# Two-layer decoder trunk: weight parts split earlier in the opening, part of the gate's modulation on TensorE, rotary embedding in two operations

## Chip, cores and metric

One core of one Trainium2 chip. The time is device microseconds (us) of one execution, median of several runs. PE is TensorE's matmul stream, PEld its weight loads, DVE VectorE, ACT ScalarE, POOL GpSimd, SP the engine whose queue issues the weight transfers.

## What is computed

Two layers of a trunk for 256 tokens of width 1024. All six modulation vectors of a layer come from one vector `c`.

```python
mod = c_act @ w_ada[l] + b_ada[l]                 # 6 x 1024 values
sh_m, sc_m, gt_m, sh_f, sc_f, gt_f = split(mod)
h = rms_norm(x, g_pre_mix[l]) * (1 + sc_m) + sh_m
proj = h @ w_in[l]                                # q, k, v of two groups; indexer q, k, weights
y = concat(rms_norm(moba(...)), rms_norm(dsa(...))) @ w_out[l]
x = x + gt_m * rms_norm(y, g_post_mix[l])
h = rms_norm(x, g_pre_ffn[l]) * (1 + sc_f) + sh_f
y = (gelu(conv(h @ w_up_act)) * (h @ w_up_lin)) @ w_down
x = x + gt_f * rms_norm(y, g_post_ffn[l])
```

With 256 tokens the MoBA group (8 heads of 64) is plain causal attention; the DSA group (8 heads) keeps for each token the 64 best keys by an indexer's score. The rotary embedding turns the first 16 elements of each head of q and k: `x1*c - x2*s`, `x2*c + x1*s`.

## The kernel before

**Numbers.** Each matmul of a projection is three matmuls: every operand is split into a high part and a low part. For a weight, ACT makes the high part `wh` (L139, or L135 with a gain) and DVE the low part `wl` (L140, L136). `wh` and `wl` have five buffers each.

**Weights.** Everything comes in one stream, in the order of the program, by 1 MB transfers on SP's queue (`load`, L112) into six buffers `raw`. A transfer is issued when the tile that had its buffer has been read, and those behind it in the queue wait too.

**Modulation.** `gemv_v` (L182) does it on DVE: one multiplication with accumulation (L189) of 128x1024 weights by the row `crow` for each group of 128 outputs, 24 of them in the first mixer: groups 16 to 23 are the gate `gt_m`, 24 to 39 are `sh_f` and `sc_f`; 40 to 47 (`gt_f`) follow in the MLP. A generator yields its gap in ticks between them, and `Background.tick` advances all such chains once for each k step of a projection. A scheduler then sets the order on each engine, so that an instruction can stand far from its line; `pin` keeps an instruction in the program's order.

**Opening** (`start`, L576). The 1024 rows of the first projection come in eight steps k of 128. Step k gets shift and scale for its 128 channels (on DVE in `modulation_v`, L650; on PE in `modulation`, L659, for k = 0, 3, 6), splits the weight row in two parts of 584 and 1024 columns (`divide`, L634), modulates the transposed tokens on ACT into `hh` (L644) and `t` (L646), and DVE makes `hl` (L647). Then PE does the step's products (L695) for the indexer (`ia`, `ib`), `mq` and `mk`.

**First mixer.** PE projects `mv`, `dq`, `dk`, `dv` (`project`, L357, two token tiles t each, matmuls L369). Chains run beside it: transposes of q and k (`heads_T`, L342; `ki_T`, L754), the indexer (L393) with its top 64 on DVE (L419, L420), both attentions (`attend`, L427, scores on DVE at L449), then the output projection into four banks (L539 to L541). `gate_rows` (L202) turns the gate into a row for all partitions by a transpose and two transfers. `boundary` (L310) closes the mixer: `residual` (L296, L304) for each token tile, the next norm (L232, L264), transposes (L252) and the modulation (`mod_T`, L275 to L287), after which PE does the MLP.

Of the kernel before, what the change touches and what calls it, by code (L numbers as in the profile page):

```python
# [13 lines left out]
AF = mybir.ActivationFunctionType  # L14
OP = mybir.AluOpType
AX = mybir.AxisListType
# [58 lines left out]
def trunk(ctx: ExitStack, tc, plan, x, c, stream, small, rope, out):  # L75
    nc = tc.nc
# [7 lines left out]
    bg = Background()  # L84
# [62 lines left out]
    rt = con.tile([128, 2, 2, 16], F32, name="rt")  # L147
# [3 lines left out]
    ident = con.tile([128, 128], F32, name="ident")  # L151
# [5 lines left out]
    cs32 = con.tile([128, 8, 32], F32, name="cs32")  # L157
# [17 lines left out]
    mods = [con.tile([128, 48], F32, name=f"mod{l}") for l in range(DEPTH)]  # L175
# [6 lines left out]
    def gemv_v(l, j0, j1, gap, behind=None):  # L182

        for j in range(j0, j1, 2):
            r = load(("v_a", l, j, 2048))[0]
            for i in range(2):
                ri = r[:, 1024 * i:1024 * i + 1024]
                with tc.issue_after(behind) if behind else ExitStack():
                    nc.vector.scalar_tensor_tensor(out=ri, in0=ri, scalar=1.0, in1=crow, op0=OP.mult, op1=OP.mult,  # L189
                                                   accum_out=mods[l][:, j + i:j + i + 1])  # L190
                yield gap
        nc.vector.tensor_tensor(out=mods[l][:, j0:j1], in0=mods[l][:, j0:j1],
                                in1=scol(l, "b_ada")[:, j0:j1], op=OP.add)

    def pre_scale(l, which):
        a = wrk.tile([128, 8], F32, name="prescale", tag="prescale", bufs=2)
        o = 8 if which == "mix" else 32
        nc.vector.scalar_tensor_tensor(out=a, in0=mods[l][:, o:o + 8], scalar=1.0,
                                       in1=scol(l, "g_pre_" + which)[:, :8], op0=OP.add, op1=OP.mult)
        return a, mods[l][:, o - 8:o]  # L200
# [128 lines left out]
    def rope_out(p, dst, t, is_q, nh):  # L329

        nc.scalar.activation(out=dst, in_=p, func=AF.Copy, scale=0.125 if is_q else 1.0)
        n = wrk.tile([128, 8, 2, 16], F32, name="ra", tag="ra", bufs=2)[:, :nh]
        x = dst[:, :, :16]

        y = bass.AP(tensor=x.tensor, offset=x.offset + 8, ap=list(x.ap[:2]) + [[-8, 2], [1, 8]])
        cosv = rt[:, t, 0, :][:, None, :].to_broadcast([128, nh, 16])
        sinv = rt[:, t, 1, :].rearrange("p (a b) -> p a b", a=2)[:, None].to_broadcast([128, nh, 2, 8])
        nc.vector.tensor_tensor(out=n[:, :, 0], in0=x, in1=cosv, op=OP.mult)
        nc.vector.tensor_tensor(out=n[:, :, 1].rearrange("p h (a b) -> p h a b", a=2), in0=y, in1=sinv, op=OP.mult)
        nc.vector.tensor_tensor(out=x, in0=n[:, :, 0], in1=n[:, :, 1], op=OP.add)  # L340

    def heads_T(src, dst, t):  # L342
        yield 5
# [232 lines left out]
    def start():  # L576
# [48 lines left out]
        halves = half_T(0), half_T(1)  # L625
# [8 lines left out]
        def divide(k, u):  # L634
            w[k, u] = split(rows[k][:, 584:] if u else rows[k][:, :584], pin=True)

        def modulate(k):
            sk, mk = scale[:, k:k + 1], mods[0][:, k:k + 1]
            pin(nc.vector.scalar_tensor_tensor(out=sk, in0=mods[0][:, 8 + k:9 + k], scalar=plus1[:, k:k + 1],
                                               in1=scol(0, "g_pre_mix")[:, k:k + 1], op0=OP.add, op1=OP.mult))  # L640
            pin(nc.vector.tensor_tensor(out=mk, in0=mk, in1=scol(0, "b_ada")[:, k:k + 1], op=OP.add))
            divide(k, 0)
            xk = xT[k // 4][:, k % 4, :]
            pin(nc.scalar.activation(out=hh[:, k, :], in_=xk, func=AF.Identity, scale=sk, bias=mk))  # L644
            f = t2()[:, :S]
            pin(nc.scalar.activation(out=f, in_=xk, func=AF.Identity, scale=sk, bias=mk))  # L646
            pin(nc.vector.tensor_tensor(out=hl[:, k, :], in0=f, in1=hh[:, k, :].bitcast(F32), op=OP.subtract))  # L647
            divide(k, 1)

        def modulation_v(k):  # L650
            for a in range(2):
# [80 lines left out]
    for l in range(DEPTH):  # L732

        qiT = big("qT")
        kiT = wrk.tile([128, S], F32, name="kiT", tag="kiT", bufs=1)
# [18 lines left out]
        def ki_T(ki, t):  # L754
            p = tp_bank()
            nc.tensor.transpose(p[:, :128], ki, ident)
            nc.vector.tensor_copy(kiT[:, 128 * t:128 * t + 128], p[:, :128])
            yield 1

        def qk_done(dst, is_q):  # L760
# [25 lines left out]
            run_project("ib", lambda t, a: idx_out(1, t, a))  # L786
            st["behind"] = placed[0]
        if l == 0:
            bg.add("gt", gemv_v(l, 16, 24, 6))
        bg.add("gt", gate_rows(l, "mix"))  # L790
        if l:
            bg.add("sf", gemv_v(l, 32, 40, 6, placed[1][1]))
# [20 lines left out]
        bg.add("att", attend(mqT, mkT, mv, None, 0, oh, ol, ready[0]))  # L813
        dqT, dkT, dv = big("qT"), big("kT"), big("v")
        if l == 0:
            bg.add("sf", gemv_v(l, 24, 40, 9))
        run_project("dq", qk_done(dqT, True))
        run_project("dk", qk_done(dkT, False))
        bg.add("att", attend(dqT, dkT, dv, masks, 4, oh, ol, ready[1]))
# [135 lines left out]
def _layout(a, plan):  # L955

    parts = []
    for units in plan:
        blocks = []
        for kind, l, key, n in units:  # L960
            if kind == "v_a":
                w = a["w_ada"][l][:, 128 * key:128 * key + 256].reshape(128, 8, 2, 128)
                b = w.transpose(3, 2, 1, 0)
            elif kind in ("s", "sv"):
                b = a["w_ada"][l][:, :2 * D].reshape(128, 8, 2, 8, 128)[:, :, :, key]
                if kind == "sv":
                    b = b.transpose(3, 2, 1, 0)
            elif kind == "r":
                b = a["w_in"][l][128 * key:128 * key + 128, sum((CCOLS[n] for n in OPEN), [])]
            elif kind in "wb":  # L970
                name, k0, k = key
                w = a["w_in" if kind == "w" else "w_up_lin"][l].reshape(8, 128, -1)[k0:k0 + k]
                b = w[:, :, CCOLS[name]].transpose(1, 0, 2)
            elif kind == "o":
                b = a["w_out"][l][128 * key:128 * key + 128]
            elif kind in "uv":
                w = a["w_up_act" if kind == "u" else "w_up_lin"][l].reshape(8, 128, FF)
                b = w[:, :, 128 * key:128 * key + 128].transpose(1, 0, 2)
            else:
                b = a["w_down"][l][128 * key:128 * key + 128]  # L980
            blocks.append(b.reshape(128, n))
        parts.append((blocks[0] if len(blocks) == 1 else np.concatenate(blocks, axis=1)).reshape(-1))
    stream = np.concatenate(parts)
    assert stream.size == STREAM
    return stream
# [13 lines left out]
def _rope_table():  # L999
    f = np.float32  # L1000
    pos = np.arange(S, dtype=f)
    inv = f(500000.0) ** (-np.arange(0, 16, 2, dtype=f) / f(16))
    ang = pos[:, None] * inv[None, :]
    co, si = np.cos(ang).astype(f), np.sin(ang).astype(f)
    cc, ss = np.concatenate([co, co], 1), np.concatenate([-si, si], 1)
    tab = np.stack([cc, ss], axis=1)
    return np.ascontiguousarray(tab.reshape(2, 128, 2, 16).transpose(1, 0, 2, 3))

# [21 lines left out]
```

## Time and profile before

| what | value |
|---|---|
| median of 3 runs | 696.31 us (695.06 to 696.6) |
| profiled execution, own time | 694.81 us |
| its span, first to last instruction | 693.0 us |
| PE busy | 662.4 us (96%) |
| DVE busy | 560.6 us (81%) |
| ACT busy | 422.4 us (61%) |
| POOL busy | 31.8 us (5%) |
| granted TensorE clock, mean | 0.994 |

The profiled execution is 1.5 us shorter than the median. Busy time is the union of an engine's instructions; consecutive instructions on DVE overlap by some 0.08 us, and consecutive matmuls overlap as well, so that a busy PE need not be one that issues without a pause.

### The profile page before, as it was taken

How to read it: one execution, taken by the hardware profiler on the slowest of the kernel's cores; microseconds unless marked ns; L12 is line 12 of the kernel's file. 1: busy time of each engine (PE TensorE's matmuls, PEld its weight loads, DVE VectorE, ACT ScalarE, POOL GpSimd, SP SyncE). 2: the span in 40 equal slices, each digit the busy share in tenths (PEclk: the TensorE clock that was granted, in tenths of full speed). 3: DMA queues.
4: the chain of work that ended last, by engine and by line, in shares of the span. 5: the costliest groups of instructions: out<-in, count | busy, mean ns of one | idle time of the engine just before them, and what ended most of it. 6: DMA issues, size and time to landing. Idle time of an engine off the chain costs nothing.

```text
span 693.0 us, 11206 instructions
## 1 busy us (share of the span) xinstructions
PE 662.4 (96%) x4257; PEld 569.1 (82%) x4257; DVE 560.6 (81%) x1130; ACT 422.4 (61%) x781; POOL 31.8 (5%) x56
## 2 busy tenths in 40 slices
PE   7999988997999999999999998999999999999996
PEld 4777766775899999999988776877789999999994
DVE  5779999999799999988669996678679886666553
ACT  5446567994865555555565657879586555555441
POOL 1000001012000000000020000000100000000000
PEclk9999999999999999999999999999999999999998
DMA  8997963766479999998444933345336895555001
GB/s 363 419 363 269 404 244 130 295 216 249 155 288 360 375 375 335 338 337 316 167 171 177 348 124 122 122 155 200 132 150 228 302 341 187 220 183 183 1 1 61
DMA packets 24517, 163.02 MB, mean 235 GB/s; under 512 B 3312, under 2 KB 3728, under 8 KB 6160
## 3 DMA queue, kind: packets, MB, share of 16 engines
q1 hardware_dynamic: 23184, 159.77, 61.2%
q0 software_dynamic: 704, 2.11, 1.0%
q8 instruction: 33, 0.54, 0.3%
q10 hardware_dynamic: 576, 0.43, 0.2%
q14 instruction: 20, 0.16, 0.1%
HBM read 161.24 MB, written 1.06 MB: 234 GB/s over the span
## 4 chain that ended last, share of the span: by engine, by line
PE 67%; DVE 18%; ACT 9%; issue 4%; POOL 1%; DMA 1%; SPq 0%; POOLq 0%; DVEq 0%; ACTq 0%
PE b L540 18%; PE b L539 18%; PE b L541 18%; PE b L369 7%; DVE raw L189 4%; DVE wl L140 3%; ACT t L453 2%; DVE iscore L420 2%; PE b L695 2%; DVE iscore L412 2%; DVE tiny L419 1%; PE b L389 1%; ACT wh L135 1%; ACT t L232 1%; PE b L468 1%
## 5 line engine op out<-in xcount | busy, mean ns | idle before, releaser
L140 DVE TENSOR_TENSOR wl<-raw,wh 128x1024 fp32r<-128x1024 f32 (+1 forms) x146 | 173.6, 1195 | 34.7 <-ACT wh L139 30.9
L539 PE MATMUL b<-hh,wh 128*128 128x256 f32 x640 | 180.0, 281 | 0.0
L541 PE MATMUL b<-hl,wh 128*128 128x256 f32 x640 | 179.7, 281 | 0.0
L540 PE MATMUL b<-hh,wl 128*128 128x256 f32 x640 | 179.7, 281 | 0.0
L139 ACT ACTIVATE wh<-raw 128x1024 fp32r<-128x1024 f32 (+1 forms) x146 | 149.2, 1045 | 45.2 <-PE b L541 36.4
L540 PEld LDWEIGHTS b<-hh,wl 128*128 128x128 f32 x640 | 122.5, 191 | 1.4
L539 PEld LDWEIGHTS b<-hh,wh 128*128 128x128 f32 x640 | 120.3, 188 | 1.4
L541 PEld LDWEIGHTS b<-hl,wh 128*128 128x128 f32 x640 | 120.1, 188 | 0.0
L189 DVE SCALAR_TENSOR_TENSOR raw<-raw,crow 128x1024 f32<-128x1024 f32 x80 | 96.2, 1219 | 1.4 <-DMA raw<-in_stream_dram 1.4
L369 PE MATMUL b<-wh,hh 128*128 128x512 f32 (+1 forms) x184 | 72.7, 397 | 0.0
L369 PE MATMUL b<-wh,hl 128*128 128x512 f32 (+1 forms) x184 | 68.5, 386 | 0.0
L139 ACT ACTIVATE dh<-raw 128x1024 fp32r<-128x1024 f32 (+2 forms) x47 | 49.7, 1059 | 25.8 <-PE b L540 25.8
L140 DVE TENSOR_TENSOR dl<-raw,dh 128x1024 fp32r<-128x1024 f32 (+2 forms) x47 | 56.8, 1210 | 8.9 <-ACT dh L139 8.9
L912 ACT ACTIVATE t<-b,smt 128x256 f32<-128x256 f32 x44 | 25.1, 571 | 57.4 <-PE b L541 57.3
L539 PE MATMUL b<-dh,t 128*128 128x512 f32 x152 | 59.7, 393 | 0.0
L540 PE MATMUL b<-dh,t 128*128 128x512 f32 x152 | 59.6, 392 | 0.0
L541 PE MATMUL b<-dl,t 128*128 128x512 f32 x152 | 59.2, 389 | 0.0
L369 PE MATMUL b<-wl,hh 128*128 128x512 f32 (+1 forms) x184 | 55.2, 391 | 2.7 <-DVE wl L140 2.7
L369 PEld LDWEIGHTS b<-wl,hh 128*128 128x128 f32 x184 | 33.9, 189 | 10.8 <-DVE wl L140 4.0
L369 PEld LDWEIGHTS b<-wh,hh 128*128 128x128 f32 x184 | 34.6, 188 | 7.3 <-issue 1.0
L369 PEld LDWEIGHTS b<-wh,hl 128*128 128x128 f32 x184 | 33.8, 188 | 5.9
L913 DVE SCALAR_TENSOR_TENSOR t<-b,smt,t 128x255 f32<-128x255 f32 x44 | 21.1, 480 | 20.7 <-ACT t L912 20.6
(167 smaller groups left out, 1105.2 us busy)
## 6 DMA issues: line engine op xcount, KB each, us to landing
raw<-in_stream_dram SPq DMA_DIRECT2D x143, 1024.0 KB, 6.5
raw<-in_stream_dram SPq DMA_DIRECT2D x8, 804.0 KB, 8.2
gate<-gated POOLq DMA_DIRECT2D x4, 512.0 KB, 7.0
xt<-in_x_dram SPq DMA_DIRECT2D x2, 512.0 KB, 4.1
raw<-in_stream_dram SPq DMA_DIRECT2D x1, 984.0 KB, 5.9
out_dram<-xt SPq DMA_DIRECT2D x2, 256.0 KB, 2.1
raw<-in_stream_dram SPq DMA_DIRECT2D x1, 328.0 KB, 5.0
out_dram<-xt ACTq DMA_DIRECT2D x1, 256.0 KB, 2.1
```

The source lines that it names most:

```text
L139: put(nc.scalar.activation(out=hi[:, :n], in_=raw, func=AF.Copy))
L140: put(nc.vector.tensor_tensor(out=lo[:, :n], in0=raw, in1=hi[:, :n].bitcast(F32), op=OP.subtract))
L189: nc.vector.scalar_tensor_tensor(out=ri, in0=ri, scalar=1.0, in1=crow, op0=OP.mult, op1=OP.mult, accum_out=mods[l][:, j + i:j + i + 1])
L369: mm = lambda l_, k, i, start=False, stop=False: nc.tensor.matmul(a[:, :n], lhsT=l_[:, k, tt], rhs=w[k][i], start=start, stop=stop)
L412: nc.vector.scalar_tensor_tensor(out=sc, in0=r[:, j * nk:j * nk + nk], scalar=wi[:, h:h + 1], in1=fill[:, 256 - nk:] if first else sc, op0 ...
L420: nc.vector.match_replace(out=sc, in_to_replace=m8, in_values=sc, imm_value=MARK)
L453: nc.scalar.activation(out=ev[:, j, :], in_=ev[:, j, :], func=AF.Exp, bias=nm[:, j:j + 1], scale=-1.0, accum_out=sm[:, j:j + 1])
L539: nc.tensor.matmul(y, lhsT=hh, rhs=wh, start=first, stop=False)
L540: nc.tensor.matmul(y, lhsT=hl, rhs=wh, start=False, stop=False)
L541: nc.tensor.matmul(y, lhsT=hh, rhs=wl, start=False, stop=last)
L912: nc.scalar.activation(out=z, in_=p[:, :256], func=AF.Identity, scale=w2[:, i:i + 1], bias=bc[:, i:i + 1])
L913: nc.vector.scalar_tensor_tensor(out=z[:, 1:], in0=p[:, :255], scalar=w1[:, i:i + 1], in1=z[:, 1:], op0=OP.mult, op1=OP.add)
```

## The change

1. **Opening.** In steps 1 to 7 the second part of the weight row (1024 columns) is split ahead of the modulation of the tokens, so that ACT and DVE do both parts first. Step 0 keeps its order.
2. **First mixer's modulation.** Groups 24 to 31 take the gate's place in the early chain on DVE (gap 6). The gate (16 to 23) goes to PE: `gemv_p` waits 34 ticks, loads two 1 MB blocks, waits 16 ticks, and then does 16 matmuls (32 columns of `cs32` stationary, 256 columns of weights moving) in a row, a copy on ACT, four transposes, and a small reduction on DVE; twice. Groups 32 to 39 stay on DVE with gap 9.
3. **Rotary embedding.** One multiplication of twice the size makes both products, and the addition reads the second with its halves exchanged. Three DVE operations become two, 14 times in each layer.
4. **`ki_T`.** The copy of the indexer's transposed keys goes from DVE to ACT, twice in each layer.

```diff
+    def gemv_p(l, j0, j1, wait, gap):
+
+        yield wait
+        for j in range(j0, j1, 4):
+            r = [load(("p", l, j + 2 * i, 2048))[0] for i in range(2)]
+            yield gap
+            p = tp_bank()
+            burst([(p[32 * (i % 4):32 * (i % 4) + 32, 256 * h:256 * h + 256], cs32[:, i, :],
+                    r[h][:, 256 * i:256 * i + 256], dict(start=i < 4, stop=i >= 4, skip_group_check=True))
+                   for h in range(2) for i in range(8)])
+            e = t2()
+            nc.scalar.activation(out=e, in_=p, func=AF.Copy)
+            yield 4
+            q = tp_bank()
+            for b in range(4):
+                nc.tensor.transpose(q[:, 128 * b:128 * b + 128], e[:, 128 * b:128 * b + 128], ident)
+            nc.vector.tensor_reduce(out=mods[l][:, j:j + 4], axis=AX.X, op=OP.add,
+                                    in_=q.rearrange("p (b g r) -> p b g r", b=4, g=4)[:, :, :, 0])
+            yield 1
+        nc.vector.tensor_tensor(out=mods[l][:, j0:j1], in0=mods[l][:, j0:j1],
+                                in1=scol(l, "b_ada")[:, j0:j1], op=OP.add)
...
-        nc.vector.tensor_tensor(out=n[:, :, 0], in0=x, in1=cosv, op=OP.mult)
-        nc.vector.tensor_tensor(out=n[:, :, 1].rearrange("p h (a b) -> p h a b", a=2), in0=y, in1=sinv, op=OP.mult)
-        nc.vector.tensor_tensor(out=x, in0=n[:, :, 0], in1=n[:, :, 1], op=OP.add)
+        nc.vector.tensor_tensor(out=n, in0=x[:, :, None, :].to_broadcast([128, nh, 2, 16]),
+                                in1=rt[:, t][:, None].to_broadcast([128, nh, 2, 16]), op=OP.mult)
...
+        nc.vector.tensor_tensor(out=halves(x), in0=halves(n[:, :, 0]), in1=y, op=OP.add)
...
             divide(k, 0)
+            if k:
+                divide(k, 1)
             xk = xT[k // 4][:, k % 4, :]
...
-            divide(k, 1)
+            if k == 0:
+                divide(k, 1)
...
-            nc.vector.tensor_copy(kiT[:, 128 * t:128 * t + 128], p[:, :128])
+            nc.scalar.copy(kiT[:, 128 * t:128 * t + 128], p[:, :128])
...
         if l == 0:
-            bg.add("gt", gemv_v(l, 16, 24, 6))
+            bg.add("sf", gemv_v(l, 24, 32, 6))
+            bg.add("gt", gemv_p(l, 16, 24, 34, 16))
...
         if l == 0:
-            bg.add("sf", gemv_v(l, 24, 40, 9))
+            bg.add("sf", gemv_v(l, 32, 40, 9))
```

The layout of the gate's blocks in the stream and the sign in the table of sines follow. The moved instructions stand as follows (line numbers of each kernel's own file).

DVE in the opening, steps 1 and 2, before:

```order
L653 SCALAR_TENSOR_TENSOR raw,mod_99<-raw,crow 128x1024 x2
L639 SCALAR_TENSOR_TENSOR prescale<-mod_99,plus_161,smt 128x1
L641 TENSOR_TENSOR mod_99<-mod_99,smt 128x1
L140 TENSOR_TENSOR wl<-raw,wh 128x584
L647 TENSOR_TENSOR hl<-t_246,hh 128x256
L140 TENSOR_TENSOR wl<-raw,wh 128x1024
```

and now:

```order
L678 SCALAR_TENSOR_TENSOR raw,mod_99<-raw,crow 128x1024 x2
L661 SCALAR_TENSOR_TENSOR prescale<-mod_99,plus_161,smt 128x1
L663 TENSOR_TENSOR mod_99<-mod_99,smt 128x1
L140 TENSOR_TENSOR wl<-raw,wh 128x584
L140 TENSOR_TENSOR wl<-raw,wh 128x1024
L671 TENSOR_TENSOR hl<-t_250,hh 128x256
```

The low part of 1024 columns now stands between the parts that ACT works on and `hl`, which needs both of them.

PE in the first mixer, second token tile of `dq` (`b_864`, before `b_875`), where the indexer's second set of products follows (`kiT`, `qT`). Before:

```order
L369 MATMUL b_875<-wl,hh 128x512 x3
L389 MATMUL b_923<-kiT,qT 128x256
L389 MATMUL b_922<-kiT,qT 128x256
L389 MATMUL b_923<-kiT,qT 128x256
L389 MATMUL b_922<-kiT,qT 128x256
L369 MATMUL b_875<-wl,hh 128x512 x3
```

and now:

```order
L411 MATMUL b_909<-raw,cs_84 32x256 x16
L391 MATMUL b_864<-wl,hh 128x512 x3
L411 MATMUL b_932<-kiT,qT 128x256
L411 MATMUL b_931<-kiT,qT 128x256
L411 MATMUL b_932<-kiT,qT 128x256
L411 MATMUL b_931<-kiT,qT 128x256
L391 MATMUL b_864<-wl,hh 128x512 x5
L210 MATMUL b_980<-ident,t_926 128x128 x4
```

The first block of the gate stands ahead of these products, its transposes behind them; the second block stands in the first token tile of `dv` in the same way.

DVE at the end of the first mixer (`o` is the last attention output, `t<-b,gate` the residual's product). Before:

```order
L534 TENSOR_TENSOR hl<-o,hh 128x4x128
L189 SCALAR_TENSOR_TENSOR raw,mod_99<-raw,crow 128x1024 x3
L296 TENSOR_TENSOR t_1749<-b_1463,gate 128x512
L192 TENSOR_TENSOR mod_99<-mod_99,smt 128x16
L296 TENSOR_TENSOR t_1750<-b_1464,gate 128x512
L198 SCALAR_TENSOR_TENSOR prescale<-mod_99,smt 128x8
L304 SCALAR_TENSOR_TENSOR xt<-t_1749,tiny_1759,xt 128x512
L304 SCALAR_TENSOR_TENSOR xt<-t_1750,tiny_1759,xt 128x512
```

and now:

```order
L318 TENSOR_TENSOR t_1778<-b_1504,gate 128x512
L556 TENSOR_TENSOR hl<-o,hh 128x4x128
L189 SCALAR_TENSOR_TENSOR raw,mod_99<-raw,crow 128x1024
L140 TENSOR_TENSOR wl<-raw,wh 128x1024
L318 TENSOR_TENSOR t_1779<-b_1505,gate 128x512
L326 SCALAR_TENSOR_TENSOR xt<-t_1778,tiny_1788,xt 128x512
L326 SCALAR_TENSOR_TENSOR xt<-t_1779,tiny_1788,xt 128x512
L189 SCALAR_TENSOR_TENSOR raw,mod_99<-raw,crow 128x1024
```

Three modulation instructions are gone from between `hl` and the residual. The two that now stand here are the first of groups 40 and 41, which before stood a little later, between the second token tile's products and `mod_T`; one `wl` of the next projection has come here too.

## Rows read from the trace of the kernel before

**Rows 1.** Windows by stage: busy us (count) by engine, granted clock, DMA share, GB/s.

```profile
0.00:57.77 57.77, 50.49 (x282) 36.97 (x282) 40.21 (x82) 31.33 (x56) 2.88 (x12) 1.00 0.96 379
57.77:112.50 54.73, 48.57 (x274) 37.07 (x272) 54.44 (x178) 35.47 (x70) 1.31 (x2) 1.00 0.65 253
112.50:163.55 51.05, 50.10 (x314) 38.28 (x314) 49.29 (x118) 40.28 (x96) 10.15 (x6) 1.00 0.74 270
163.55:183.32 19.77, 15.22 (x68) 12.11 (x69) 14.88 (x29) 14.87 (x37) 3.12 (x6) 0.91 0.28 104
```

**Rows 2.** Timeline of DVE, opening, step 1: start, us, instruction, idle before and its releaser.

```profile
17.50 0.76 DVE L140 TENSOR_TENSOR wl<-raw,wh 128x584 fp32r<-128x584 f32 x1
18.75 0.42 DVE L647 TENSOR_TENSOR hl<-t,hh 128x256 fp32r<-128x256 f32 x1 [0.49 <-ACT t L646]
19.70 1.23 DVE L140 TENSOR_TENSOR wl<-raw,wh 128x1024 fp32r<-128x1024 f32 x1 [0.53 <-ACT wh L139]
...
23.46 0.76 DVE L140 TENSOR_TENSOR wl<-raw,wh 128x584 fp32r<-128x584 f32 x1
```

**Rows 3.** Timeline of ACT, opening, start of step 2.

```profile
23.58 0.60 ACT L644 ACTIVATE hh<-xT,mod,prescale 128x256 fp32r<-128x256 f32 x1 [3.33 <-DVE mod L641]
```

**Rows 4.** Timeline of PE, opening: first products of steps, a modulation, the mixer's start.

```profile
18.28 0.42 PE L695 MATMUL b<-wh,hh 128*128 128x328 f32 x1
...
41.30 0.42 PE L695 MATMUL b<-wh,hh 128*128 128x328 f32 x1
...
42.57 1.07 PE L664 MATMUL b<-raw,cs 128*32 128x256 f32 x16
...
47.41 0.31 PE L695 MATMUL b<-wh,hh 128*128 128x328 f32 x1
...
49.19 0.50 PE L695 MATMUL b<-wl,hh 128*128 128x512 f32 x1 [0.30 <-DVE wl L140]
...
52.44 0.42 PE L695 MATMUL b<-wh,hh 128*128 128x328 f32 x1
...
57.77 0.39 PE L369 MATMUL b<-wh,hh 128*128 128x512 f32 x1
```

**Rows 5.** PE's waits from 57.77 to 112.6 us: total, times, longest.

```profile
PE b L369 <- DVE wl L140: 2.7, 3, 1.6
PE b L346 <- DVE t L340: 1.4, 2, 0.9
```

**Rows 6.** Groups of DVE, 57.77 to 163.55 us: busy us, mean ns of one, idle before.

```profile
L189 DVE SCALAR_TENSOR_TENSOR raw<-raw,crow 128x1024 f32<-128x1024 f32 x24 | 28.8, 1220 | 0.0
...
L494 DVE TENSOR_TENSOR t<-t 128x256 f32<-128x256 f32 x2 | 0.8, 419 | 0.0
```

**Rows 7.** Timeline of DVE, first mixer: two operations of the rotary embedding.

```profile
62.53 0.28 DVE L338 TENSOR_TENSOR ra<-t,rt 128x128 f32<-128x128 f32 x1
62.73 0.29 DVE L340 TENSOR_TENSOR t<-ra 128x128 f32<-128x128 f32 x1
```

**Rows 8.** Timeline of DVE, end of the first mixer.

```profile
161.51 0.69 DVE L296 TENSOR_TENSOR t<-b,gate 128x512 f32<-128x512 f32 x1
...
162.87 0.75 DVE L304 SCALAR_TENSOR_TENSOR xt<-t,tiny,xt 128x512 f32<-128x512 f32 x1
...
168.81 1.21 DVE L189 SCALAR_TENSOR_TENSOR raw<-raw,crow 128x1024 f32<-128x1024 f32 x1
```

**Rows 9.** Timeline of PE, end of the first mixer: transposes and the waits before them.

```profile
155.37 0.32 PE L528 MATMUL b<-ident,tiny 128*128 128x128 f32 x1 [0.81 <-POOL tiny L525]
...
166.80 1.97 PE L252 MATMUL b<-ident,t 128*128 128x128 f32 x8 [3.26 <-DVE t L264]
...
175.22 1.10 PE L252 MATMUL b<-ident,t 128*128 128x128 f32 x8 [0.39 <-DVE t L264]
```

**Rows 10.** Window of two us after that wait (columns as in rows 1).

```profile
167.00:169.00 2.00, 2.00 (x9) 1.87 (x9) 2.00 (x5) 1.04 (x3) 0.56 (x1) 0.50 0.02 8
```

**Rows 11.** Weight transfers issued from 60 to 130 us: issue to landing, min, median, max.

```profile
DMA to landing us min/median/max: 4.7/6.7/8.3
```

More of the change, by code (lines that the diff above doesn't have):

```diff
@@ L333, in rope_out @@
         x = dst[:, :, :16]
-        y = bass.AP(tensor=x.tensor, offset=x.offset + 8, ap=list(x.ap[:2]) + [[-8, 2], [1, 8]])
-        cosv = rt[:, t, 0, :][:, None, :].to_broadcast([128, nh, 16])
-        sinv = rt[:, t, 1, :].rearrange("p (a b) -> p a b", a=2)[:, None].to_broadcast([128, nh, 2, 8])
-        nc.vector.tensor_tensor(out=n[:, :, 0], in0=x, in1=cosv, op=OP.mult)
-        nc.vector.tensor_tensor(out=n[:, :, 1].rearrange("p h (a b) -> p h a b", a=2), in0=y, in1=sinv, op=OP.mult)
-        nc.vector.tensor_tensor(out=x, in0=n[:, :, 0], in1=n[:, :, 1], op=OP.add)
+        nc.vector.tensor_tensor(out=n, in0=x[:, :, None, :].to_broadcast([128, nh, 2, 16]),
+                                in1=rt[:, t][:, None].to_broadcast([128, nh, 2, 16]), op=OP.mult)
+        y = n[:, :, 1]
+        y = bass.AP(tensor=y.tensor, offset=y.offset + 8, ap=list(y.ap[:2]) + [[-8, 2], [1, 8]])
+        halves = lambda v: v.rearrange("p h (a b) -> p h a b", a=2)
+        nc.vector.tensor_tensor(out=halves(x), in0=halves(n[:, :, 0]), in1=y, op=OP.add)
     def heads_T(src, dst, t):
@@ L963, in _layout @@
                 b = w.transpose(3, 2, 1, 0)
+            elif kind == "p":
+                b = a["w_ada"][l][:, 128 * key:128 * key + 256].reshape(128, 8, 256)
             elif kind in ("s", "sv"):
@@ L1004, in _rope_table @@
     co, si = np.cos(ang).astype(f), np.sin(ang).astype(f)
-    cc, ss = np.concatenate([co, co], 1), np.concatenate([-si, si], 1)
+    cc, ss = np.concatenate([co, co], 1), np.concatenate([si, -si], 1)
     tab = np.stack([cc, ss], axis=1)
```

## Prediction

> **What bounds the kernel now.** I read the windows by stage first, then the timelines of the engines that are full there, then the waits. Over the whole span PE is 96% busy, so a change helps where PE stands still or where another engine paces it. Rows 1 give four stages. In the opening (to 57.77 us) PE is busy 50.49 us and DVE 40.21, though it is the stage in which weights come at 379 GB/s. In the first part of the mixer (`mv`, `dq`, `dk` and the indexer, to 112.50) DVE is busy 54.44 of 54.73 us and PE only 48.57. In the second part (to 163.55) both are nearly full, PE 50.10 and DVE 49.29 of 51.05. At the boundary (to 183.32) PE is busy 15.22 of 19.77, at a mean granted clock of 0.91 [rows 1].
>
> What paces the opening shows on DVE: a step lasts from 17.50 to 23.46, 5.96 us, of which 0.49 is a wait for `t` from ACT and 0.53 one for `wh` from ACT; the work is 4.94 [rows 2]. ACT for its part stands 3.33 us until DVE has the next step's modulation [rows 3]. The two hand the step back and forth, and neither is full. PE follows them.
>
> **The opening: −3.8 us.** With both low parts ahead of `hl`, DVE works on 1024 columns (1.23 us) while ACT makes `hh` (0.60) and `t`, and ACT has split those columns while DVE did the 584. Both waits go, so DVE needs 4.94 us for a step. Then PE is next: from 41.30 to 47.41 a step with a modulation on PE took 6.11 us (two times eight matmuls of the modulation lie in such a step, 1.07 us for each eight), from 47.41 to 52.44 one without took 5.03, of which 0.30 is a wait, so 4.7 of work [rows 4]. From the start of step 1 at 18.28, five steps of 4.7 and two of 6.1 are 35.7 us, which puts the start of `mv` at 54.0 instead of 57.77 [rows 4]. If DVE's 4.94 holds in the five and PE's sequence has gaps, 1.3 to 1.8 less is gained; if PE's step has slack I don't see, a little more: ends −4.5 and −2.
>
> **First part of the mixer: 0.** Here two things are set against each other. PE stands still for 54.73 − 48.57 = 6.16 us [rows 1], of which 2.7 is waiting for a low part of a weight and 1.4 for rotated heads, both from DVE [rows 5]. DVE is relieved. Ahead of the first low part of `dv` stand 11 modulations by the new order, 13 by the old: two of 1.22 fewer, 2.4 [rows 6]. Fourteen rope operations go at a pitch of 0.20 each (62.53 to 62.73) [rows 7], but the product that replaces them is twice as wide: the nearest row is an operation of 128x256 at 0.42 against 0.28 for 128x128 [rows 6, 7], so 0.14 is paid and 0.06 saved, 14 times 0.8. Two copies of `ki_T` are bounded by the same pitch, 0.4, and a small reduction takes 0.1 back. Together 3.5 us. But the modulations used to fill DVE's time while the indexer waits for its scores; with fewer of them there, I expect most of it (2.7 to 3.5) to return as idle time of DVE. And PE gets the first burst: 16 matmuls of 256 columns at about 1.0 us for eight [rows 4] are 2.0 to 2.1, and the four transposes and the change of stationary operands 0.8 (a modulation step's 6.11 less 4.7 less 1.07 leaves 0.4 for two) [rows 4], together 2.8. It falls into PE's 6.16 of idle time where this lies near, else on the path. Ends −3.4 (the whole relief) and +2.8 (the whole burst); I take 0, since the indexer's chain and not DVE's sum decides here.
>
> [...]
>
> **Second part: +2.0.** PE is busy 50.10 of 51.05 us [rows 1], so the second burst's 2.8 lies on the path. What it may displace is the wait of 0.81 at 155.37 for a small operand from POOL [rows 9], which is over earlier when PE comes later: 2.8 − 0.8. Behind the burst on ACT stand a copy and the split of the output weights; if a transfer they wait for has been issued late, the landing of 4.7 (the least of [rows 11]) comes on top: ends +1.9 and +7.5.
>
> **Boundary: −3.4.** Between `hl` of the last output and the residual DVE has three modulations less. The last sum stands at 162.87, 1.36 behind the first product at 161.51 [rows 8], and one modulation and a `wl` are still there, which the new order puts ahead of the second product only; I take −1.4. One modulation at 168.81 of 1.21 [rows 8], ahead of `mod_T`, is moved off: −1.1, the pitch. And PE's wait of 3.26 before the first transposes is followed by 1.97 us for eight of them, the second eight taking 1.10 [rows 9]; the granted clock from 167 to 169 is 0.50, the lower level, after that wait [rows 10]. With a shorter wait I take the difference of 0.9 as gained. Ends −5 (all of it and a part of the remaining wait) and −0.5 (the moved instructions only change place).
>
> **Layer 1: −0.4.** The rope and the copies relieve DVE by 1.3 us as above; PE is nearly always full in that mixer, so a third of it. Ends −1.1 and 0.
>
> **Sum.** −3.8 + 0 + 2.0 − 3.4 − 0.4 = −5.6. The profiled execution would go from 694.81 to 689.2; the median of the runs lies 1.5 above the profiled one, so the median from 696.31 to **690.7**.
>
> **Rivals.**
> - *DVE paces the first mixer throughout.* For it: 54.44 of 54.73 busy. Then the relief of 3.5 shows in full and the burst falls wholly into PE's idle time, and about 1.1 more comes from the second part; the gain is 10.2 and the time 686.1. Against it: more than half of PE's idle time there is not put down to a low part [rows 5]. Chance 0.15.
> - *The stream bounds the opening.* The DMA share is 0.96 at 379 GB/s [rows 1]. If weights land just in time, a faster step only waits for its weights: the −3.8 goes, and with a little of the rest the time is 694.5. Against it: 57.77 us at 379 GB/s are 21.9 MB, while the tokens (1.05 MB), eight steps (0.82 and 1.05 each) and `mv` (2.1) need 18.1; the stream is 3.8 MB ahead, 10 us at that rate. Chance 0.07. [...]
> - *The longer ring, slower than before.* The four 1 MB blocks of the gate are held from their load through a wait of 16 ticks, two at a time, so that four buffers instead of six serve all else, and `dv` comes later in the stream. A transfer that waits for a buffer holds up the whole queue behind it; where a late landing is at the head of an in-order engine (ACT's split of the output weights behind the second burst, DVE's low parts before the boundary), each costs 4.7 to 8.3 us [rows 11]. It ends slower than before once such waits exceed 5.6 and the change's own uncertainty, some 7 us in all. Two such landings of 4.7 give 9.4 − 5.6 = +3.8, 700.1. Against it: the DMA share in these parts is 0.65 and 0.74 [rows 1], so the stream has room to catch up. Chance 0.10.
> - *The mixer gives the opening back.* Both bursts lie on the path (5.6) and the boundary gains only 1: −3.8 + 2.8 + 1.9 − 1.0 − 0.4 = −0.5, about 695.8. Chance 0.08.
>
> **How the numbers follow.** The forecast has 0.60. Its own range, from the ends of the terms taken a part at a time, is 687 to 694. The range is 685.0 to 696.5: below it takes in the rival in which DVE paces all, above it the stream and the mixer that gives the opening back; what is left out is the longer ring and a tenth of the others. A measurement of this kernel can tell about 0.2%, 1.4 us. Faster by more than this are the forecast and the first rival and most of the stream's case: 0.81 (0.60 + 0.15 + 0.06); within it lie the mixer that gives back and the rest, 0.09; slower is the longer ring, 0.10.
>
> **What would show it.** In the opening, DVE without the two waits in steps 1 to 7 and the start of `mv` near 54; if it stays near 57, the stream or PE's order is the bound. In the first part, PE's idle time between `mv` and the first low part of `dv`, and whether DVE now has idle time that it had not. The bursts at about 2.1 us each, with what PE did just ahead and behind; a burst that waits for its block would be the longer ring. At the boundary, the residual's last sum within 1.5 us of its first product, no modulation ahead of `mod_T`, the granted clock of the first transposes, and the MLP's start, 183.32 before, near 178. It is wrong if the opening gains under 2, if a landing shows as the releaser of a wait of over 2 us in the mixer, or if DVE fills the mixer and PE's idle time goes altogether.

## The result, and the profile after

| | kernel before | changed kernel |
|---|---|---|
| median, runs on the same chip | 695.06 us | 690.69 us (690.61 to 692.22, 5 runs) |
| ratio, 95% interval | | 0.9939 [0.9924, 0.9955] |
| profiled execution, span | 693.0 us | 688.8 us |
| PE busy, DVE busy | 662.4, 560.6 us | 665.3, 551.5 us |

The change saves 4.4 us by the medians and 4.2 us by the two spans. The forecast was 690.7 us from a median of 696.31; the kernel before took 695.1 to 695.3 in the runs beside which everything below was timed, so the forecast gain of 5.6 was 1.2 too large and the start 1.2 too high. Which terms of the sum hold is seen by stage.

The windows by stage of the changed kernel (start:end, length, then busy us and count of PE, PEld, DVE, ACT, POOL, granted clock, DMA share, GB/s); they answer to [rows 1], with the same borders: `mv`'s first product, the first product of `dv` with a low part, the last output product, the MLP's first product.

```profile
0.00:52.75 52.75, 48.74 (x281) 37.52 (x282) 39.25 (x90) 31.26 (x55) 2.88 (x12) 1.00 0.98 399
52.75:108.41 55.66, 51.68 (x309) 38.02 (x308) 52.29 (x150) 34.02 (x69) 0.00 (x0) 1.00 0.74 273
108.41:162.39 53.98, 53.08 (x351) 39.58 (x351) 46.98 (x113) 46.16 (x108) 6.34 (x9) 1.00 0.68 255
162.39:178.88 16.49, 14.11 (x69) 10.98 (x69) 12.11 (x25) 12.87 (x33) 3.05 (x6) 1.00 0.25 93
```

| stage | before | after | difference | forecast |
|---|---|---|---|---|
| opening | 57.77 | 52.75 | −5.0 | −3.8 |
| first part of the mixer | 54.73 | 55.66 | +0.9 | 0 |
| second part | 51.04 | 53.98 | +2.9 | +2.0 |
| boundary | 19.78 | 16.49 | −3.3 | −3.4 |
| the rest, layer 1 in it | 509.68 | 509.92 | +0.2 | −0.4 |
| span | 693.0 | 688.8 | −4.2 | −5.6 |

DVE's timeline in the opening, step 1 (start, us, instruction; idle time before it in brackets), answers to [rows 2]:

```profile
17.51 1.90 DVE L140 TENSOR_TENSOR wl<-raw,wh 128x584 fp32r<-128x584 f32 x2
19.32 0.42 DVE L671 TENSOR_TENSOR hl<-t,hh 128x256 fp32r<-128x256 f32 x1
...
22.27 1.90 DVE L140 TENSOR_TENSOR wl<-raw,wh 128x584 fp32r<-128x584 f32 x2
```

Both low parts now stand in one row, neither of the two waits of half a microsecond is left, and the step takes 4.76 us instead of 5.96. PE paces the opening instead. Its timeline there, first products of steps 3 to 6, answers to [rows 4]:

```profile
28.94 0.31 PE L720 MATMUL b<-wh,hh 128*128 128x328 f32 x1
...
33.33 0.31 PE L720 MATMUL b<-wh,hh 128*128 128x328 f32 x1
...
37.71 0.32 PE L720 MATMUL b<-wh,hh 128*128 128x328 f32 x1
...
43.51 0.31 PE L720 MATMUL b<-wh,hh 128*128 128x328 f32 x1
```

A step without a modulation is 4.39 us, one with it 5.80. The stream of weights is close behind: from 10 to 50 us it moves 418 GB/s, and ACT now waits three times for a weight to land (1.9 us in all, the longest below), which it never did in the opening before. PE is not held up by it, with 38.43 of 40.00 us busy.

```profile
10.00:50.00 40.00, 38.43 (x233) 31.39 (x231) 32.50 (x66) 24.40 (x41) 0.00 (x0) 1.00 1.02 418
```

```profile
29.36 1.65 ACT L139 ACTIVATE wh<-raw 128x584 fp32r<-128x584 f32 x2 [0.90 <-DMA raw<-in_stream_dram]
```

The bursts on PE, in the timeline of PE:

```profile
80.47 1.93 PE L411 MATMUL b<-raw,cs 128*32 128x256 f32 x32
...
85.57 0.60 PE L210 MATMUL b<-ident,t 128*128 128x128 f32 x4
...
91.03 0.44 PE L368 MATMUL b<-ident,t 128*128 128x128 f32 x2 [1.72 <-DVE t L362]
...
110.47 1.93 PE L411 MATMUL b<-raw,cs 128*32 128x256 f32 x32
...
163.81 1.09 PE L274 MATMUL b<-ident,t 128*128 128x128 f32 x8 [1.42 <-DVE t L286]
```

Neither burst waits for its block. The last row answers to the first two of [rows 9]: the wait ahead of the first transposes is 1.42 instead of 3.26 us, and the eight take 1.09 instead of 1.97; the granted clock of the boundary is 1.00, where it was 0.91.

What had not been there is idle time of DVE in the mixer. DVE, 64 to 71 us:

```profile
64.34 1.23 DVE L189 SCALAR_TENSOR_TENSOR raw<-raw,crow 128x1024 f32<-128x1024 f32 x1
...
68.37 2.36 DVE L140 TENSOR_TENSOR wl<-raw,wh 128x1024 fp32r<-128x1024 f32 x2 [2.79 <-ACT wh L139]
```

and ACT, which makes those high parts, at the same time:

```profile
65.82 0.60 ACT L795 ACTIVATE v<-b 128x512 f32<-128x512 f32 x1 [1.27 <-PE b L391]
66.31 0.58 ACT L369 COPY qT<-b 128x512 f32<-128x512 f32 x1
66.78 0.60 ACT L369 COPY kT<-b 128x512 f32<-128x512 f32 x1
67.25 1.08 ACT L139 ACTIVATE wh<-raw 128x1024 fp32r<-128x1024 f32 x1
```

The weights for `dq` stand on ACT behind three copies of PE's results, of which the first waited 1.27 us for PE. DVE has done all that it was given and stands still for 2.79 us, and it needs the time later: from there to the end of its indexer work (the second mask) it is busy 38.21 of 38.79 us. The mask, in the second row below, ends at 107.16, only 1.5 us earlier than the 108.63 of the kernel before, although `mv` starts 5.0 us earlier.

```profile
68.37:107.16 38.79, 35.25 (x212) 25.22 (x214) 38.21 (x124) 23.75 (x47) 0.00 (x0) 1.00 0.67 242
```

```profile
106.73 0.43 DVE L446 TENSOR_TENSOR mask<-mask,lateneg 128x256 f32<-128x256 f32 x1
```

### The profile page after: what moved, and what is told of

Same layout as the page of the kernel before. It is cut to its first block, busy times and chain, and to the rows that moved or that the text cites. A ratio compares the mean times of both kernels' runs of the same rounds, so it can differ in the third digit from the quotient of the medians.

```text
span 688.8 us, 11311 instructions
## 1 busy us (share of the span) xinstructions
PE 665.3 (97%) x4329; PEld 570.3 (83%) x4329; DVE 551.5 (80%) x1085; ACT 424.8 (62%) x787; POOL 26.6 (4%) x56
## 4 chain that ended last, share of the span: by engine, by line
PE 75%; DVE 11%; ACT 7%; issue 3%; POOL 1%; DMA 1%; SPq 0%; POOLq 0%; DVEq 0%; ACTq 0%
PE b L563 18%; PE b L562 18%; PE b L561 18%; PE b L391 11%; DVE wl L140 3%; PE b L720 3%; PE b L411 2%; ACT t L475 2%; DVE iscore L442 1%; PE b L490 1%; DVE tiny L441 1%; ACT t L254 1%; DVE iscore L434 1%; DVE raw L678 1%; DMA raw<-in_stream_dram 1%
## 5 line engine op out<-in xcount | busy, mean ns | idle before, releaser
L189 DVE SCALAR_TENSOR_TENSOR raw<-raw,crow 128x1024 f32<-128x1024 f32 x72 | 86.8, 1220 | 0.4 <-DMA raw<-in_stream_dram 0.2
```

## The experiments

Twelve kernels ran, in three groups of four. The first question was whether the parts of the change add, each in its own stretch (theory A), or whether the mixer takes the opening's gain back (B) or is paced by DVE (C). Ratios are against the kernel before, beside the same runs. The stages are of each kernel's profiled execution: "to the mask" is from `mv`'s first product to the end of the second mask on DVE, "to the outputs" from there to the last output product.

| kernel | median us | ratio, interval | `mv` at | to the mask | to the outputs | boundary | rest |
|---|---|---|---|---|---|---|---|
| before | 695.1 to 695.3 | | 57.77 | 50.86 | 54.91 | 19.8 | 509.7 |
| changed | 690.69 | 0.9939 [0.9924, 0.9955] | 52.75 | 54.41 | 55.23 | 16.5 | 509.9 |
| opening only | 694.53 | 0.9984 [0.9974, 0.9994] | 52.90 | 54.61 | 55.11 | 18.2 | 511.8 |
| gate only | 693.08 | 0.9965 [0.9953, 0.9978] | 57.73 | 50.30 | 57.81 | 15.8 | 509.4 |
| changed, gate on DVE | 695.99 | 1.0011 [0.9997, 1.0024] | 53.07 | 55.60 | 56.00 | 20.2 | 513.9 |
| changed, old rotary and copy | 690.64 | 0.9925 [0.9913, 0.9936] | 53.00 | 54.32 | 55.62 | 15.8 | 509.4 |
| changed, old opening | 696.45 | 1.0011 [1.0002, 1.0020] | 57.83 | 50.62 | 59.58 | 15.6 | 511.1 |
| rotary and copy only | 696.81 | 1.0019 [1.0005, 1.0032] | 57.73 | 53.15 | 60.47 | 15.1 | 510.1 |
| changed, earlier modulation | 689.08 | 0.9908 [0.9892, 0.9924] | 53.04 | 53.89 | 55.11 | 15.4 | 509.9 |
| changed, later burst | 692.37 | 0.9961 [0.9944, 0.9978] | 52.74 | 52.42 | 60.17 | 15.0 | 509.8 |
| opening, earlier modulation | 692.09 | 0.9959 [0.9948, 0.9971] | 53.01 | 52.92 | 56.09 | 18.5 | 511.6 |
| changed, gap 5 | 689.39 | 0.9919 [0.9907, 0.9931] | 52.87 | 53.37 | 55.76 | 15.7 | 509.9 |
| changed, gaps 5 and 13 | 689.20 | 0.9920 [0.9907, 0.9933] | 52.69 | 52.19 | 56.06 | 15.6 | 510.0 |
| copy only | 694.64 | 0.9996 [0.9982, 1.0009] | 57.73 | 51.30 | 57.46 | 15.3 | 509.8 |

A profiled execution can lie off the median of its kernel. That of "changed, gate on DVE" was the longest of its twelve, 4.5 us above their median, so its stages are too long in all; "opening, earlier modulation" lies 1.8 and "rotary and copy only" 1.6 above, "copy only" 1.2 below. The others lie within 0.8.

### The opening alone

```diff
             divide(k, 0)
+            if k:
+                divide(k, 1)
...
-            divide(k, 1)
+            if k == 0:
+                divide(k, 1)
```

> The kernel before with the opening's new order alone. Theory A, the parts act each in its own stretch and their gains add: mv starts near 52.75 us as in the changed kernel (57.77 before), and nearly all of the 5.0 us reaches the end, so the time is 4 to 5 us under the kernel before, about 0.993 of it, with the boundary still lasting 19.8 us and the transposes there at the lower clock. Rival B, the first mixer gives the opening back whoever makes it earlier (its modulations and weights come no sooner, so PE waits for them): mv near 52.75 but the output projection starts no more than 2.5 us earlier than 129.99, and the time is 0 to 2.5 us under the kernel before.

Measured: `mv` at 52.90, the time 0.6 us under the kernel before, 0.9984 of it. Theory A is gone: of 4.9 us at `mv`, 1.1 are left at the second mask (107.51 against 108.63), 0.9 at the last output product, 2.5 at the MLP's first product and by the span 0.4 at the end. Rival B's numbers hold (0 to 2.5, and the output projection starts 1.9 earlier), but not its reason: of 4.7 us of PE's waits up to the mask, 4.2 are put down to DVE and 0.5 to a weight's high part on ACT. DVE's side, by windows from `mv` to the mask, before and here:

```profile
57.77:108.63 50.86, 46.51 (x254) 35.70 (x254) 50.84 (x167) 31.60 (x58) 1.31 (x2) 1.00 0.70 272
```

```profile
52.90:107.51 54.61, 49.65 (x254) 36.40 (x254) 52.55 (x157) 33.57 (x60) 1.31 (x2) 0.95 0.72 268
```

PE does the same 254 matmuls, 3.1 us slower, with a mean granted clock of 0.95 (the last section has the place; DVE was busy throughout it, so the mask was not held up by it). DVE was busy 50.84 of 50.86 us before; here it is busy 52.55 of 54.61: 1.7 us of work more in that stretch (among it one modulation more ahead of the mask by the instructions' order, 13 for 12), and 2.06 idle, nearly all of it one wait:

```profile
68.73 2.36 DVE L140 TENSOR_TENSOR wl<-raw,wh 128x1024 fp32r<-128x1024 f32 x2 [1.95 <-ACT wh L139]
```

Together 3.75 of the 4.87 us gained. The boundary gave 1.6 us, and the MLP took 2.1 back: PE waits once, at its beginning, for DVE, where it did not before. On DVE a low part more stands ahead of each of the two operations that this matmul needs (`t`, L916 and L918; before, L913 and L915); first PE, then DVE, then DVE before:

```profile
188.53 0.36 PE L539 MATMUL b<-hh,wh 128*128 128x256 f32 x1 [1.58 <-DVE t L918]
```

```profile
185.20 1.22 DVE L140 TENSOR_TENSOR wl<-raw,wh 128x1024 fp32r<-128x1024 f32 x1
186.34 0.48 DVE L916 SCALAR_TENSOR_TENSOR t<-b,smt,t 128x255 f32<-128x255 f32 x1
186.77 1.23 DVE L140 TENSOR_TENSOR wl<-raw,wh 128x1024 fp32r<-128x1024 f32 x1
187.91 0.48 DVE L918 SCALAR_TENSOR_TENSOR t<-b,smt,t 128x254 f32<-128x254 f32 x1
```

```profile
187.92 0.48 DVE L913 SCALAR_TENSOR_TENSOR t<-b,smt,t 128x255 f32<-128x255 f32 x1
188.43 0.48 DVE L915 SCALAR_TENSOR_TENSOR t<-b,smt,t 128x254 f32<-128x254 f32 x1
```

The second of them comes 7.1 us after the MLP's first product, and 5.1 before. Of the fourteen kernels three have this wait, 1.58 or 1.60 us long: the three with the new opening and the gate on DVE.

### The gate alone

`gemv_p`, its two places in the chains and its blocks in the stream as in the change, all else as before.

> The kernel before with the gate's modulation on PE alone. Theory A: mv starts at 57.8; the mixer from there to the last output product becomes 2 to 4 us longer (PE work of 6.1 us comes in, of which the old idle time takes 2 to 4), the boundary 3.3 shorter than 19.8 us; the time is between 1.5 under and 1 us over the kernel before. Rival C, DVE paces the mixer and the relief of DVE pays for the bursts: the mixer is no longer than 105.8 us and the time is 3 us or more under the kernel before.

Measured: 2.1 us under the kernel before. The mixer is 2.3 us longer (108.1 against 105.8), within theory A's 2 to 4, the boundary 4.0 shorter; the total is somewhat better than A's bound of 1.5, and C's 3 is not reached.

### The change without the gate, and without the rotary embedding

The change with one part put back: first the gate's modulation on DVE (groups 16 to 23 with gap 6, then 24 to 39 with gap 9), then the three-operation rotary embedding and the `ki_T` copy on DVE.

> The changed kernel with the gate's modulation back on DVE: opening, rotary embedding and ki_T copy as changed. Theory A: the opening's 5.0 and up to 1 us of the rotary embedding are kept, the boundary goes back to 19.8 us; 4.5 to 6 us under the kernel before, so as fast as the changed kernel or up to 1.5 us faster. Rival B, the gate's move is what carries the gain at the boundary and the opening is given back: 2 to 4 us slower than the changed kernel.

> The changed kernel with the three-operation rotary embedding and ki_T on DVE as before. Theory A, the rotary embedding was worth next to nothing, since DVE has 5 us of idle time more in the changed mixer: within 1 us of the changed kernel. Rival C, DVE paces the first mixer: 2 us slower than the changed kernel or more.

Without the gate's move nothing is left of the gain: 1.0011, with "no difference" inside its interval. Rival B had the direction, but it is 5.3 us slower than the change where B asked for 2 to 4; 1.5 of this lies between it and the opening alone (694.53), to which it adds the rotary embedding and the copy. Opening alone gives 0.6, the gate alone 2.1, both 4.5 (the kernel with the old rotary embedding): the opening is worth 2.4 us once the gate is off DVE, and 0.6 otherwise. By the stages this difference is not made in the mixer. There the opening's gain shrinks in both settings, to 0.7 us at the mask with the gate on PE (107.33 against 108.02) and 1.1 with it on DVE, and at the MLP's first product it is 2.9 us (178.78 against 181.63) and 2.5 (180.79 against 183.32). What sets them apart is above all the MLP's wait shown above; why the scheduler placed the low parts so is open. And the rotary embedding is worth nothing in the changed kernel, 690.64 without it and 690.69 with it, as A had expected. These two kernels have the same number of modulations and low parts ahead of each score and each mask by their orders, so this compares the operations themselves.

### Two more combinations

The change with the old opening (first), and the rotary embedding and the copy alone. The theory by now, D: DVE's queue sets when the first part of the mixer ends.

> The changed kernel with the opening's old order (gate on PE, rotary embedding and ki_T as changed). Theory D, formed after the first four runs: DVE's queue sets when the first part of the mixer ends (its second mask is done at 107.2 to 108.7 us in every kernel so far), so time is made by DVE work taken out ahead of that point; with the old opening DVE has no idle time in the mixer, so the shorter rotary embedding shows and the time is about 1 us under the kernel with the gate alone on PE, near 692.0. Rival E, the rotary embedding is worth nothing in any setting: within 0.4 us of the kernel with the gate alone, 693.1.

> The kernel before with the two-operation rotary embedding and the ki_T copy on ACT alone. Theory D: DVE is busy 54.44 of 54.73 us there, so the relief of some 1.3 us in the first mixer reaches the end: 693.5 to 694.3. Rival E, worth nothing: 694.8 to 695.6. It made the kernel 1.4 us slower when it was added to the new opening alone; if that holds here too, 696 or more.

Both missed D and E: 696.45 and 696.81, slower than the kernel before by intervals that exclude "no difference" (for the second this is what the last sentence of its expectation had, if the earlier loss repeated). Yet DVE has less to do. In the second of them the mask comes at 110.88, 2.3 us later than before; by the orders 13 modulations and 11 low parts of 1024 columns stand ahead of it, 12 and 10 before. Shortening an operation gave the scheduler another order, with two operations of 1.2 us ahead of the work that the mixer waits for. That the order is what costs was not isolated further; the operations alone cost nothing, as the pair above shows. A rival for the outputs' 60.47 us is the clock: in the profiled execution it was at the lower level in three stretches of the mixer, some 14 us in all, of which the longest is this:

```profile
154.90:161.80 6.90, 6.74 (x29) 5.57 (x30) 4.39 (x8) 0.76 (x3) 0.13 (x1) 0.51 0.72 258
```

The two are not separated. In the first of the two kernels the mask is 0.4 us later than with the gate alone (108.45 against 108.02), and most of the loss lies behind it, in the outputs (59.58 against 57.81) and the rest; why there is open.

### Filling DVE's idle time

```diff
-            bg.add("sf", gemv_v(l, 24, 32, 6))
+            bg.add("sf", gemv_v(l, 24, 32, 4))
```

> The changed kernel with the gap of the first modulation chain (groups 24 to 31) 4 ticks instead of 6, so that eight instead of six of its multiplications stand ahead of the indexer's first score, where DVE had an idle time of 2.79 us (65.6 to 68.4). Theory D: two multiplications of 1.22 us go into idle time and DVE's second mask comes up to 2.4 us earlier: 1 to 2.4 us under the changed kernel, 688.3 to 689.7. Rival F, PE's own work now sets the mixer's length: within 0.5 us of the changed kernel.

The same edit on the opening alone, where the chain is the gate's (6 to 4):

> The kernel before with the opening's new order, and the gap of the gate's chain 4 ticks instead of 6: eight instead of six multiplications stand ahead of the indexer's first score, as many as before ahead of its second mask. Theory D: the opening's gain was lost because DVE ran dry for 1.95 us at 66.8 us and had more to do later; filling that gives 1 to 2 us: 692.5 to 693.5 (694.53 with the gap of 6). Rival F, it was lost on PE or in the stream of weights: within 0.5 us of 694.5.

Both times came out as D says: 1.6 us under the changed kernel (2.2 by the ratios, whose intervals touch), and 2.4 us under the opening alone, a little more than its range (1.7 by the ratios, whose intervals are apart). DVE's timeline of the changed kernel with gap 4, at the place of the 2.79 us:

```profile
65.77 1.23 DVE L189 SCALAR_TENSOR_TENSOR raw<-raw,crow 128x1024 f32<-128x1024 f32 x1
...
66.91 1.23 DVE L189 SCALAR_TENSOR_TENSOR raw<-raw,crow 128x1024 f32<-128x1024 f32 x1
...
68.74 0.35 DVE L434 SCALAR_TENSOR_TENSOR iscore<-t,wi,fill 128x128 f32<-128x128 f32 x1 [0.59 <-ACT t L431]
```

Two modulations fill it, and the indexer's score follows. But D had expected the mask up to 2.4 us earlier, and it comes only 0.2 earlier (106.92 against 107.16): thirteen modulations are done ahead of it now, and eleven in the changed kernel. The gain shows behind it, most of it at the boundary (15.4 against 16.5 us). There no modulation and no low part is left between `hl` and the residual's sums, which come at 157.10 instead of 159.89, and PE's wait of 1.42 us ahead of the first transposes is gone:

```profile
157.10 1.42 DVE L326 SCALAR_TENSOR_TENSOR xt<-t,tiny,xt 128x512 f32<-128x512 f32 x2 [0.34 <-POOL tiny L264]
```

```profile
162.10 1.09 PE L274 MATMUL b<-ident,t 128*128 128x128 f32 x8
```

So the number was D's, and the way to it was not. For the opening with gap 4, the window from `mv` to the mask:

```profile
53.01:105.93 52.92, 47.77 (x254) 36.01 (x254) 52.71 (x157) 32.62 (x60) 1.31 (x2) 0.98 0.74 276
```

DVE does the same work as with gap 6 (52.71 and 52.55), but idles 0.21 us instead of 2.06, and the mask comes 1.6 us earlier. So much of the opening's loss up to the mask is shown: an engine that is full later had been left without work earlier. How the 1.6 becomes 2.4 us at the end is not shown, since in the profiled execution, which lies above the median, 0.6 of it are left at the last output product and 0.5 at the end, and the MLP's wait of 1.6 us is still there.

### The burst at another place, and finer gaps

First the gate's chain 8 ticks later (`gemv_p(l, 16, 24, 42, 16)`).

> The changed kernel with the gate's chain 8 ticks later, so that the first burst no longer stands between the indexer's products but nearer to PE's wait of 1.72 us at 91 us. Theory D: the indexer's second scores come 1.9 us earlier but DVE is behind anyway: within 0.7 us of the changed kernel. Rival F, PE's work and waits set the mixer's length: the burst fills the wait and 1 to 1.7 us are gained.

Missed by both: 692.37, 1.7 us slower than the change by the medians, with intervals that overlap. The mask is 2.0 us earlier (105.17), and from there to the last output product it takes 4.9 us longer, with new waits of PE. The waits of PE from 105 to 166 us in that kernel (total, times, longest):

```profile
PE b L543 <- DVE ss L518: 1.6, 1, 1.6
PE b L391 <- DVE wl L140: 1.3, 1, 1.3
PE b L562 <- DVE hl L556: 1.0, 1, 1.0
PE b L561 <- ACT hh L555: 0.9, 1, 0.9
```

So the mask alone does not set the mixer's end: what follows has waits of its own. Then gap 5 for the first chain, and with it gap 13 for the second:

> The changed kernel with the gap of the first chain 5 ticks: eight multiplications ahead of the first score as with 4, but eight instead of ten ahead of the second score and twelve instead of thirteen ahead of the second mask. Theory D: another 0.5 to 1.2 us under the kernel with 4, 687.8 to 688.6. Rival F, PE is the bound by now: 688.8 to 689.5.

> As the kernel before this one, and the second chain's gap 13 ticks instead of 9, so that eleven instead of twelve multiplications stand ahead of the second mask and the others come later, nearer to the boundary. Theory D: 0.3 to 1.2 us less in the mixer, of which the boundary can take back up to 1.2 where a multiplication falls between the residual's products: 687.0 to 689.0. Rival F: 689 to 690.

689.39 and 689.20, the same as gap 4 within the intervals; the masks come 0.7 and 2.0 us earlier, but less of it arrives. Both lie in rival F's range, though that PE is the bound by now is not shown by it. With DVE's idle time filled, taking more from it ahead of the mask no longer pays. Gap 4 is the fastest by its median, 6.2 us under the kernel before.

Last the copy alone:

> The kernel before with the ki_T copy on ACT alone. Theory D: by the scheduler's order thirteen instead of twelve multiplications stand ahead of the second mask, so it is 0.3 to 1.2 us slower than the kernel before although DVE has 0.4 us less to do. Rival E, the relief counts: 0 to 0.4 us faster.

694.64, no difference from the kernel before (0.9996 [0.9982, 1.0009]). The median is 0.5 us lower, about as rival E had it. D's count, one modulation more ahead of the mask, had asked for a loss; the mask is indeed 0.4 us later (109.03), the stretch to the last output product 2.6 longer, and the boundary 4.5 shorter. Counting what stands ahead of the mask is no forecast of the end.

## Why the prediction was right or wrong

**What bounds the kernel** was read rightly for the opening: the two waits of DVE went, PE became the next bound. The size of the term (−3.8) was too small because PE's step was taken from rows that still held pauses, 4.7 and 6.1 us. PE's undisturbed steps are 4.39 and 5.80. Five and two of them are 33.6, and 0.9 us in all is lost at steps where PE still waits; 52.75 is what comes. One reading in the working is wrong without touching the sum: a step holds eight matmuls of the modulation once and not twice (the 16 records of 1.07 us in [rows 4] are these eight; the gate's 16 have 32 records and 1.93 us).

**First part of the mixer, 0.** Right as a net of the changed kernel (+0.9), and its parts went the way that was said: DVE's relief came back as idle time, 3.4 us (52.29 of 55.66 busy), against the 2.7 to 3.5 forecast. But the sum put the opening's −3.8 and this 0 side by side as if they were independent. This addition is the weak step: it takes the opening's gain at `mv` for a gain at the end, and the opening alone is worth 0.6 us there. Once the gate is off DVE it is worth 2.4, which is still only about half of the 5.0 at `mv`. The rival "the mixer gives the opening back" had a chance of 0.08 with two bursts on PE as its mechanism; the runs show DVE instead, running dry ahead of the mask and, with the gate on it, late in the MLP.

**Second part, +2.0:** +2.9. The burst and its transposes are 1.9 and 0.6 us, a little under the 2.0 and 0.8 taken; yet PE's busy time in the whole mixer grew by 6.1 us (98.67 to 104.76) where 5.6 were forecast, and its idle time fell by 2.2. PE's wait of 0.81 for POOL shrank to 0.30, nearly as forecast.

**Boundary, −3.4:** −3.3, and for the reasons given, with other sizes. DVE's timeline there answers to [rows 8]:

```profile
159.29 0.68 DVE L318 TENSOR_TENSOR t<-b,gate 128x512 f32<-128x512 f32 x1
159.89 1.41 DVE L326 SCALAR_TENSOR_TENSOR xt<-t,tiny,xt 128x512 f32<-128x512 f32 x2
161.21 1.22 DVE L189 SCALAR_TENSOR_TENSOR raw<-raw,crow 128x1024 f32<-128x1024 f32 x1
...
164.95 1.37 DVE L300 TENSOR_SCALAR t<-b,prescale,mod 128x128 f32<-128x128 f32 x4 [0.18 <-PE b L274]
```

The residual's sums come 3.0 us earlier (162.87 to 159.89) while PE's last product comes 1.1 earlier, so 1.8 of PE's wait are gone where 1.4 were taken. The modulation that is left (161.21) stands where DVE would wait anyway, and none stands ahead of `mod_T` any more. The clock drop after the long wait is gone, and with it the 0.9. That leaves 0.6 for the modulation ahead of `mod_T`, where 1.1 were taken. What the forecast did not see is that a boundary is also short when PE is merely late: the two kernels with the copy, or the copy and the rotary embedding, alone have it at 15.3 and 15.1 us, behind outputs that end 3 to 8 us later than before.

**Layer 1, −0.4:** +0.2 for all that follows the boundary, just outside the bounds of −1.1 and 0. The rotary embedding shortens a rope from three pitches of 0.20 us to 0.33 + 0.20 (in DVE's timeline of the changed kernel two multiplications start at 54.20 and the additions behind them at 54.86), some 0.07 less, and at the end this is worth nothing (690.69 with it, 690.64 without).

**The rivals.** "DVE paces the first mixer throughout" fits the first part in the kernel before, where DVE idles 0.3 us, and not in the changed one, where it idles 3.4. The stream did not bound the opening: it moved 399 GB/s, more than before, and `mv` came 5.0 us earlier; but with 418 GB/s at a DMA share of 1.02 in its middle, and ACT waiting 1.9 us for landings, by the author's estimate from these numbers little of it is left. No burst waited for its block, and no wait of PE, DVE or ACT in the mixer is put down to a landing, so the longer ring cost nothing that shows.

**The number** itself, 690.7, agrees by luck, since the errors of its terms cancel: the opening was 1.2 too small, the mixer 1.8 too good, the rest 0.6 too good, and the kernel before was 1.2 us faster beside these runs than in those shown.

## What to carry to other kernels

A gain on one engine need not reach the end: here 5.0 us at `mv` were 1.5 at the mask, in part because DVE, full in the next stage, had no work to start on earlier. So ask of such an engine not only how busy it is, but what it will have to do in the time that becomes free. Where it would run dry, pull deferrable work (here modulations, by one number of a chain) into that place; this was worth 2.4 us with the opening alone and 1.6 on top of the change. Where a scheduler sets the order, a change can also give another order elsewhere: the cheaper rotary embedding alone came out 1.5 us slower (whether by its order was not isolated), and the opening alone lost 1.6 us in a wait behind two operations in the MLP, a stage that it does not touch. So each part is timed alone and together, and followed to the end of the kernel.

## What the runs showed of the hardware

The granted clock did not follow the length of PE's last wait alone. In the kernel before, 3.26 us of idle were followed by transposes at the lower level [rows 9, 10]. In the opening alone PE's wait at the boundary was 2.62 us, and the transposes behind it ran at the full clock, 1.09 us; but the clock fell right after them, to 0.50 until about 170 us, so that the boundary's mean is 0.91 in both kernels. In the mixer of the opening alone the clock was at the lower level from 102 to about 108 us, after a stretch in which PE was busy 0.90 of 2.70 us. Windows of that kernel, and PE's rows:

```profile
98.00:100.70 2.70, 0.90 (x4) 0.39 (x4) 2.70 (x19) 2.36 (x11) 0.00 (x0) 1.00 0.93 306
...
102.00:104.00 2.00, 1.28 (x5) 0.72 (x5) 2.00 (x9) 1.64 (x2) 0.00 (x0) 0.50 0.09 37
...
106.00:108.00 2.00, 1.96 (x14) 1.66 (x16) 2.00 (x10) 1.41 (x3) 0.00 (x0) 0.50 0.00 0
108.80:110.00 1.20, 1.18 (x12) 0.69 (x8) 1.20 (x3) 1.20 (x5) 0.00 (x0) 1.00 0.00 0
...
166.50:168.00 1.50, 1.50 (x4) 1.21 (x5) 1.50 (x6) 1.50 (x6) 0.63 (x1) 0.56 0.28 38
168.00:170.00 2.00, 2.00 (x6) 1.51 (x6) 2.00 (x5) 2.00 (x7) 0.00 (x0) 0.50 0.84 324
```

```profile
103.23 1.11 PE L468 MATMUL b<-ident,t 128*128 128x128 f32 x4 [0.72 <-DVE t L461]
...
111.53 0.66 PE L468 MATMUL b<-ident,t 128*128 128x128 f32 x4 [0.22 <-ACT o L492]
...
165.23 1.09 PE L252 MATMUL b<-ident,t 128*128 128x128 f32 x8 [2.62 <-DVE t L264]
```

At the lower level four transposes took 1.11 us, and 0.66 at the full clock. The changed kernel has a wait of 1.72 us in the mixer and one of 1.42 at the boundary and kept the full clock in both. So such a place cost more than PE's wait there, since the transposes behind it took 1.7 times as long.
